# A planner that knows the SBUF port shared by VectorE and GpSimd, and three gate blocks early, two held back

## The chip, the cores and the metric

The kernel runs on one core of a Trainium2 chip. The metric is the device time of one execution, in microseconds. Names used below: TensorE (PE in the profile) multiplies matrices and transposes, VectorE (DVE) and ScalarE (ACT) do elementwise work, GpSimd (POOL) does elementwise work too, and SyncE (SP) issues nearly all DMA transfers.

## The reference

One encoder block over a sequence of 1024 positions and 1024 channels, in float32.

```python
h = rmsnorm(x, norm_w) * (1 + scale) + shift          # scale, shift, gate from silu(c) @ w_ada
proj = h @ w_in                                       # split into the parts below
ya = (a_cg * dwconv3(a_bg * a_x) * silu(a_z)) @ w_pa
q, k, v = split(silu(dwconv5(concat(q, k, v))))       # 8 heads of 128 channels
q, k = l2norm(q), l2norm(k)
o = gated_delta(q, k, v, g, beta) + flip(gated_delta(flip(q), flip(k), flip(v), ...))
yb = (headnorm(o) * gdn_norm_w * silu(z_b)) @ w_pb
merged = sigmoid(gate_a_raw) * ya + sigmoid(gate_b_raw) * yb
y = rmsnorm(x + gate * (merged @ w_o), final_norm_w)
```

The gated delta rule updates a 128x128 state per head and direction, chunk by chunk. In a chunk it needs the inverse of a lower triangular matrix that is built from the products of the keys.

## The kernel before

Every large product is made from a high and a low part of both factors: three matmuls (high by high, high by low, low by high) for each of eight 128-row slices, on halves of 512 positions. A *block* is the product of 128 output channels for all 1024 positions, 48 matmuls. Its weights arrive by DMA in two pieces; ScalarE rounds each to the high part (`wh_...`) and GpSimd subtracts to get the low part (`wl_...`).

The kernel has three stages.

1. The start: x is loaded, normalised, transposed and modulated; the first blocks k0, q0, v0 are made. In the profile this is about the first 99 us.
2. The heads, to about 821 us. For each head h: blocks q, k, v and z of the input projection; a five-tap convolution of q, k and v on VectorE (`conv5`, 1024 columns per instruction) and a Silu on ScalarE; `prep_k` (transposes `ktp`, decay matrices `D`, products `gram`, the matrices `N`); the inversion of the 32x32 diagonal blocks on GpSimd, 60 short instructions on tiles `E` and `et` with data brought in and out by DMA (`N<-s`, `Vb<-s`); `merge` (transposes of `N` and `Vb` into `T`, `y`, products `psy`, `psu`, `psz`, `psv`), which joins the blocks to 128x128 inverses; `prep_q` (`qk`, `qtp`, `vtp`); `chain`, eight steps in two directions at once, each step running cb, r (VectorE), cb, vw (ScalarE), cb, S (VectorE); the normalisation of the output (`oss`, `vp`) and `head_out` (`otp`, and a store).
3. The rest, written in program order: four blocks of gate b, the gated convolution mixer, the output products, the last norm.

In the first two stages the order of instructions is planned when the program is built. Generators (`chain`, `merge`, `head_out`, `prep_k`, `prep_q`, and `fill` for the blocks) yield their TensorE instructions; every VectorE, ScalarE, GpSimd and DMA instruction is recorded as an `Op` with an estimated cost (`Engine.cost`) and its dependences. `Scheduler.run` keeps an estimated clock for TensorE (`t`) and a time at which each other engine is free (`free`), and always issues what can start first; among instructions that are ready on an engine, the one with the smaller priority number and older number goes first. The resulting order on every engine is fixed. On the chip each engine runs its queue in that order and waits where an operand is late. TensorE takes the streams in the order in which they are listed, chains first and blocks last.

`fill` decides which block comes next, one block ahead of the one in work:

```python
share = (total - START - RESERVE) * (mains - len(jobs)) / mains + START
if gates and jobs and total - len(gates) < int(share):
    return gates.pop(0)
if jobs and (len(gates) <= RESERVE or all(n in sched.done for n in jobs[0][3])):
    return jobs.pop(0)
return gates.pop(0) if gates else None
```

`gates` are eight blocks of gate a, ga0 to ga7 (a Sigmoid on ScalarE and a store follow each). `jobs` are 27 blocks of the heads, in the order k2, v1, z0, then q, k, v, z for the heads that follow (q2, k3, v2, z1, and so on), and at the end q7, v7, z6, z7. Each has conditions: q and k wait for a chain two heads back, v for the queries of the head before, z for a head's output. With START = 4 and RESERVE = 4 the order is q1, ga0 to ga3, all 27 jobs, ga4 to ga7.

The functions that the change touches, with what calls them:

Of the kernel before, what the change touches and what calls it, by code (L numbers as in the profile page):

```python
# [21 lines left out]
NEG = -1.0e30  # L22

A_BG, A_CG, A_X, A_Z, Q0, K0, V0, Z0, G_A, G_B = (8 * i for i in range(10))
START = 4
RESERVE = 4
PLAIN = (0, 4)
LAST = 6
AHEAD = 5
# [9 lines left out]


class Op:
    def __init__(self, engine, issue, cost, extra, table, prio, seq):
        self.engine, self.issue, self.cost, self.extra, self.table = engine, issue, cost, extra, table
        self.key, self.ready, self.left, self.after = (prio, seq), 0.0, 0, []


# [8 lines left out]
class Scheduler:  # L55
# [9 lines left out]
    def __init__(self, pe):  # L65
        self.pe, self.t, self.prio, self.seq = pe, 0.0, 2, 0
        self.where, self.count, self.slots = {}, {}, {}
        self.free, self.queue, self.table, self.waiting = {}, {}, None, 0
        self.done, self.held, self.busy = set(), set(), {}

    @contextmanager
# [36 lines left out]
        parts = [self.slots[slot, i] for i in range(4) if (slot, i) in self.slots]  # L108
        return not any(s.reads or s.writes or s.fills for s in parts)

    def record(self, engine, issue, outs, ins, cost, extra, table, fill):
        op = Op(engine, issue, cost, extra, table, self.prio, self.seq)
        self.seq += 1
        op.reads = [s for ap in ins for s in self.parts(ap)]
        op.writes = [s for ap in outs for s in self.parts(ap)]
        op.fill = fill
        deps = set()
        for s in op.reads:
            op.ready = max(op.ready, self.after(engine, s.write, s.fill))
            deps.update(s.writes, s.fills)  # L120
        for s in op.writes:
            op.ready = max(op.ready, self.after(engine, s.read, s.fill))
            deps.update(s.reads, s.fills)
            if fill:
                op.ready = max(op.ready, self.after(engine, s.write))
                deps.update(s.writes)
        op.left = len(deps)
        for d in deps:
            d.after.append(op)
        for s in op.reads:  # L130
            s.reads.append(op)
        for s in op.writes:
            (s.fills if fill else s.writes).append(op)
        self.waiting += 1
        if not op.left:
            self.queue.setdefault(engine, []).append(op)

    def issue(self, op, at):
        load = 1.28 if op.table and op.table != self.table else 0.0
        self.table = op.table or self.table  # L140
        op.issue()
        self.free[op.engine] = at + op.cost + load
        end = at + op.cost + load + op.extra
        for s in op.reads:
            s.reads.remove(op)
            s.read[op.engine] = max(s.read.get(op.engine, 0.0), end)
        for s in op.writes:
            if op.fill:
                s.fills.remove(op)
                s.fill[op.engine] = max(s.fill.get(op.engine, 0.0), end)  # L150
            else:
                s.writes.remove(op)
                s.write[op.engine] = max(s.write.get(op.engine, 0.0), end)
        for d in op.after:
            d.left -= 1
            d.ready = max(d.ready, end + self.hop(op.engine, d.engine))
            if not d.left:
                self.queue.setdefault(d.engine, []).append(d)
        self.waiting -= 1
# [102 lines left out]
class Engine:  # L262
# [4 lines left out]

    def cost(self, op, outs, ins, kw):

        n = outs[0].free_size() / 1000.0  # L270
        if self._name == "dma":
            size = min(outs[0].nbytes(), ins[0].nbytes())
            return max(0.4, size / 360e3), 2.4 + size / 500e3
        if self._name == "act":
            pointers = sum(isinstance(kw.get(k), bass.AP) for k in ("bias", "scale"))
            return 0.1 + 0.83 * n + 0.07 * pointers + 0.12 * (len(outs) > 1), 0.08
        if self._name == "pool":
            if ALU.pow in kw.values():
                return 1.7, 0.1
            return (0.31 + 1.95 * n if "tensor" in op else 0.06 + 0.7 * n), 0.05  # L280
        if op == "transpose":
            return 0.16 + 1.1 * n, 0.03
        both = sum(i.space != PSUM and i.free_size() == outs[0].free_size() for i in ins) > 1
        fast = op in ("tensor_copy", "tensor_scalar", "memset") and ins and ins[0].space != PSUM
        return 0.07 + 0.06 * (op == "scalar_tensor_tensor") + (0.66 if fast else 1.16 if both else 1.04) * n, 0.07

    def __getattr__(self, op):
        real = getattr(self._engine, op)

        def call(*args, **kw):  # L290
            aps = [x for x in args if isinstance(x, bass.AP)]
            outs = aps[:1] + [kw[k] for k in ("out", "accum_out") if k in kw]
            ins = aps[1:] + [v for k, v in kw.items() if k not in ("out", "accum_out") and isinstance(v, bass.AP)]
            outs = [o for o in outs if o is not None]
            table = next((x for x in args if x in (AF.Silu, AF.Exp, AF.Sigmoid)), None) if self._name == "act" else None
            cost, extra = self.cost(op, outs, ins, dict(enumerate(args), **kw))
            self._sched.record(self._name, lambda: real(*args, **kw), outs, ins, cost, extra, table, op == "memset")  # L297

        return call

# [2 lines left out]
def block(ctx: ExitStack, tc: tile.TileContext, x, cT, wada, wadag, badaT, nwT, win, wab, cva, cvq,  # L303
# [773 lines left out]
    def fill():  # L1077
# [14 lines left out]
        def choose():  # L1092
# [6 lines that stand above are left out]
# [501 lines left out]
```

## Time and profile before

| | us |
|---|---|
| median of 3 runs | 1506.59 |
| lowest and highest of them | 1505.53, 1507.33 |
| the profiled execution, its own time | 1503.92 |
| its span, first to last instruction | 1502.1 |
| busy in the span: TensorE | 1409.6 |
| VectorE | 856.0 |
| ScalarE | 612.3 |
| GpSimd | 678.8 |

The busy time of an engine is the time in which at least one of its instructions runs. "PEclk", and the column after the engines in a table by stage, is the clock that TensorE was granted, as a part of full speed. In rows of groups, "x8 | 17.2, 2150 | 35.9" means eight instructions, 17.2 us of busy time together, 2150 ns each in the mean, and 35.9 us in which the engine stood idle just before them. In rows of waits, the numbers are the total in us, the count and the longest. In rows of the timeline, the first number is the start in us, the second the duration, and a bracket gives the idle time before it and what ended it; "x2" is two instructions merged into one row.

### The profile page before, as it was taken

To read this page: it belongs to the slowest core of one execution; us is meant where nothing else is said; L and a number is where in the kernel's file an instruction comes from. 1 tells how busy PE (TensorE), PEld (TensorE's weight loads), DVE (VectorE), ACT (ScalarE), POOL (GpSimd) and SP (SyncE) were. 2 spreads that over 40 slices of the span, in tenths; PEclk is the share of its full clock that TensorE was granted. 3 is DMA by queue.
4 is the path that set the end of the run, shared out by engine and by line. 5 is a ranking of instruction groups with operands and counts; after the bars stand their busy time and mean duration, and the time that the engine had idled before them with its cause. 6 is when DMAs were issued, how large, how long until landed. Compare 5 with 4: busy or idle time off the path is not lost.

```text
span 1502.1 us, 22636 instructions
## 1 busy us (share of the span) xinstructions
PE 1409.6 (94%) x8526; PEld 1164.2 (78%) x8526; DVE 856.0 (57%) x1467; ACT 612.3 (41%) x1493; POOL 678.8 (45%) x864
## 2 busy tenths in 40 slices
PE   4899898999899898989999999999999999999998
PEld 3777677878678786868787878787877787788886
DVE  6969075575656757476424636575667455623335
ACT  5229636456554646365433332222222341222211
POOL 5213756635637273643713554455555412255301
PEclk9999899999999999999999999999999999999999
DMA  8323241224122232323212220303031276655502
GB/s 300 99 88 105 74 131 32 82 72 127 43 72 80 51 108 49 95 71 99 56 44 85 98 99 29 112 28 113 29 106 35 93 258 229 225 191 168 197 14 99
DMA packets 123581, 153.37 MB, mean 102 GB/s; under 512 B 74704, under 2 KB 75088, under 8 KB 123472
## 3 DMA queue, kind: packets, MB, share of 16 engines
q1 hardware_dynamic: 123184, 151.14, 31.6%
q8 instruction: 67, 1.10, 0.3%
q10 hardware_dynamic: 288, 0.79, 0.1%
q14 instruction: 42, 0.34, 0.1%
HBM read 122.40 MB, written 29.49 MB: 101 GB/s over the span
## 4 chain that ended last, share of the span: by engine, by line
PE 44%; DVE 7%; POOL 2%; ACT 2%; issue 1%; POOLq 0%; ACTq 0%
PE ps_ax_S L1233 3%; PE ps_cg_S L1233 3%; PE pp_ga L206 3%; PE ps_bg_S L1233 3%; PE ps_az_S L1233 2%; PE pp_pb L1137 2%; PE pp_pb L1138 2%; PE pp_pb L1139 2%; PE fo L1506 2%; PE fo L1504 2%; PE fo L1505 2%; DVE ga L1438 2%; PE pp_gb L1137 1%; PE pp_gb L1138 1%; PE pp_gb L1139 1%; PE ps_ax_A L1233 1%
## 5 line engine op out<-in xcount | busy, mean ns | idle before, releaser
L297 POOL TENSOR_TENSOR et<-E 128x30 f32<-128x30 f32 (+7 forms) x240 | 111.3, 464 | 26.7 <-DMA E<-s 9.4
L297 POOL TENSOR_TENSOR E<-E,et 128x30 f32<-128x30 f32 (+7 forms) x240 | 109.6, 457 | 17.8
L297 ACT ACTIVATE vw<-cb,cols 128x128 f32<-128x128 f32 x112 | 35.7, 365 | 114.7 <-PE cb L206 114.6
L297 DVE SCALAR_TENSOR_TENSOR S<-S,exps,cb 128x128 f32<-128x128 f32 x96 | 29.3, 342 | 80.8 <-PE cb L206 80.2
L297 DVE SCALAR_TENSOR_TENSOR N<-gram,cols,D 128x128 f32<-128x128 f32 x128 | 34.6, 342 | 48.1 <-PE gram L206 48.1
L297 POOL TENSOR_TENSOR wl_q<-wr_q,wh_q 128x512 fp32r<-128x512 f32 x16 | 24.0, 1504 | 77.9 <-ACT wh_q L297 71.6
L206 PE MATMUL pp_ga<-hhi,wh_ga 128*128 128x512 f32 x128 | 53.2, 415 | 5.0 <-ACT wh_ga L297 5.0
L1129 POOL TENSOR_TENSOR wl_pa<-wr_pa,wh_pa 128x512 fp32r<-128x512 f32 x16 | 20.7, 1310 | 80.7 <-ACT wh_pa L1128 80.7
L206 PE MATMUL pp_z<-hhi,wh_z 128*128 128x512 f32 x128 | 55.0, 430 | 0.0
L206 PE MATMUL pp_z<-hlo,wh_z 128*128 128x512 f32 x128 | 54.4, 425 | 0.0
L206 PE MATMUL pp_z<-hhi,wl_z 128*128 128x512 f32 x128 | 54.0, 422 | 0.0
L206 PE MATMUL pp_ga<-hhi,wl_ga 128*128 128x512 f32 x128 | 53.0, 414 | 1.0 <-POOL wl_ga L297 0.8
L297 POOL TENSOR_TENSOR wl_ga<-wr_ga,wh_ga 128x512 fp32r<-128x512 f32 x16 | 22.9, 1441 | 68.4 <-PE pp_ga L206 33.2
L206 PE MATMUL pp_ga<-hlo,wh_ga 128*128 128x512 f32 x128 | 52.7, 412 | 0.0
L297 ACT ACT_TABLE_LOAD x40 | 51.3, 1283 | 1.4 <-PEq L1595 0.8
L1137 PE MATMUL pp_pb<-bhi,wh_pb 128*128 128x512 f32 x128 | 50.6, 396 | 0.0
L1139 PE MATMUL pp_pb<-bhi,wl_pb 128*128 128x512 f32 x128 | 50.6, 395 | 0.0
L1138 PE MATMUL pp_pb<-blo,wh_pb 128*128 128x512 f32 x128 | 50.6, 395 | 0.0
L1137 PE MATMUL pp_pa<-yhi,wh_pa 128*128 128x512 f32 x128 | 50.5, 394 | 0.0
L1138 PE MATMUL pp_pa<-ylo,wh_pa 128*128 128x512 f32 x128 | 49.9, 389 | 0.0
L1139 PE MATMUL pp_pa<-yhi,wl_pa 128*128 128x512 f32 x128 | 49.8, 389 | 0.0
L297 DVE SCALAR_TENSOR_TENSOR r<-cb,negeg,vp 128x128 f32<-128x128 f32 x112 | 34.4, 345 | 25.9 <-PE cb L206 25.0
(807 smaller groups left out, 4695.7 us busy)
## 6 DMA issues: line engine op xcount, KB each, us to landing
wada<-in_wada SPq DMA_DIRECT2D x16, 512.0 KB, 6.9
D<-gr_d SPq DMA_DIRECT2D x16, 512.0 KB, 5.9
xt<-in_x SPq DMA_DIRECT2D x8, 512.0 KB, 8.3
wr_k<-in_win SPq DMA_DIRECT2D x16, 256.0 KB, 3.3
wr_q<-in_win SPq DMA_DIRECT2D x16, 256.0 KB, 3.7
wr_v<-in_win SPq DMA_DIRECT2D x16, 256.0 KB, 4.3
wr_ga<-in_win SPq DMA_DIRECT2D x16, 256.0 KB, 3.0
qg<-er_d SPq DMA_DIRECT2D x8, 512.0 KB, 5.5
```

The lines of the kernel that those rows point to most:

```text
L206: getattr(self.pe, what)(out, *ins, **kw)
L297: self._sched.record(self._name, lambda: real(*args, **kw), outs, ins, cost, extra, table, op == "memset")
L1129: G.tensor_tensor(lo[:, ch(q, 512)], raw, hi[:, ch(q, 512)].bitcast(F32), ALU.subtract)
L1137: PE.matmul(ps, wh, mhi[k][:, sl], start=i == 0, stop=False)
L1138: PE.matmul(ps, wh, mlo[k][:, sl], start=False, stop=False)
L1139: PE.matmul(ps, wl, mhi[k][:, sl], start=False, stop=i == KT - 1)
L1233: PE.matmul(ps, w[:, ch(m)], r, start=first and m == i == 0, stop=m == 3 and i == 2, skip_group_check=True)
L1438: V.scalar_tensor_tensor(ga, wt[:, d, :], sc_t[:, d : d + 1], ga, ALU.mult, ALU.add)
L1504: PE.matmul(ps, mhi[k][:, ch(t)], wh, start=k == 0, stop=False)
L1505: PE.matmul(ps, mlo[k][:, ch(t)], wh, start=False, stop=False)
L1506: PE.matmul(ps, mhi[k][:, ch(t)], wl, start=False, stop=k == KT - 1)
```

## The change

The planner gets one time for the shared port, `Scheduler.port`. An instruction that uses the port starts no earlier than that time and moves it to its own end. On GpSimd every instruction of more than 30 columns uses it, but memsets and powers do not. On VectorE an instruction of more than 30 columns uses it if it has two full-size SBUF inputs, or if it is a copy or an operation with scalars on one SBUF input. The cost constants of GpSimd and of VectorE's two-input instructions are set anew. START goes from 4 to 3 and RESERVE from 4 to 2. What the kernel computes, its instructions and their sizes stay as they are; only their order can differ.

```diff
-START = 4
-RESERVE = 4
+START = 3
+RESERVE = 2
...
 class Op:
-    def __init__(self, engine, issue, cost, extra, table, prio, seq):
-        self.engine, self.issue, self.cost, self.extra, self.table = engine, issue, cost, extra, table
+    def __init__(self, engine, issue, cost, extra, table, port, prio, seq):
+        self.engine, self.issue, self.cost, self.extra, self.table, self.port = engine, issue, cost, extra, table, port
...
-        self.free, self.queue, self.table, self.waiting = {}, {}, None, 0
+        self.free, self.queue, self.table, self.waiting, self.port = {}, {}, None, 0, 0.0
...
         op.issue()
+        if op.port:
+            at = max(at, self.port)
+            self.port = at + op.cost
         self.free[op.engine] = at + op.cost + load
         end = at + op.cost + load + op.extra
...
         if self._name == "dma":
             size = min(outs[0].nbytes(), ins[0].nbytes())
-            return max(0.4, size / 360e3), 2.4 + size / 500e3
+            return max(0.4, size / 360e3), 2.4 + size / 500e3, False
         if self._name == "act":
             pointers = sum(isinstance(kw.get(k), bass.AP) for k in ("bias", "scale"))
-            return 0.1 + 0.83 * n + 0.07 * pointers + 0.12 * (len(outs) > 1), 0.08
+            return 0.1 + 0.83 * n + 0.07 * pointers + 0.12 * (len(outs) > 1), 0.08, False
         if self._name == "pool":
             if ALU.pow in kw.values():
-                return 1.7, 0.1
-            return (0.31 + 1.95 * n if "tensor" in op else 0.06 + 0.7 * n), 0.05
+                return 1.62, 0.1, False
+            return (0.28 + 1.93 * n if "tensor" in op else 0.06 + 0.7 * n), 0.05, op != "memset" and n > 0.03
         if op == "transpose":
-            return 0.16 + 1.1 * n, 0.03
+            return 0.16 + 1.1 * n, 0.03, False
         both = sum(i.space != PSUM and i.free_size() == outs[0].free_size() for i in ins) > 1
         fast = op in ("tensor_copy", "tensor_scalar", "memset") and ins and ins[0].space != PSUM
-        return 0.07 + 0.06 * (op == "scalar_tensor_tensor") + (0.66 if fast else 1.16 if both else 1.04) * n, 0.07
+        return (0.07 + 0.06 * (op == "scalar_tensor_tensor") + (0.66 if fast else 1.08 if both else 1.04) * n, 0.07,
+                bool(both or fast) and n > 0.03)
```

`record` and `__getattr__` hand the new value `port` from `cost` to `Op`. `n` is the number of columns in thousands.

More of the change, by code (lines that the diff above doesn't have):

```diff
@@ L109, in clear, with record @@
         return not any(s.reads or s.writes or s.fills for s in parts)
-    def record(self, engine, issue, outs, ins, cost, extra, table, fill):
-        op = Op(engine, issue, cost, extra, table, self.prio, self.seq)
+    def record(self, engine, issue, outs, ins, cost, extra, table, fill, port):
+        op = Op(engine, issue, cost, extra, table, port, self.prio, self.seq)
         self.seq += 1
@@ L295, in call @@
             table = next((x for x in args if x in (AF.Silu, AF.Exp, AF.Sigmoid)), None) if self._name == "act" else None
-            cost, extra = self.cost(op, outs, ins, dict(enumerate(args), **kw))
-            self._sched.record(self._name, lambda: real(*args, **kw), outs, ins, cost, extra, table, op == "memset")
+            cost, extra, port = self.cost(op, outs, ins, dict(enumerate(args), **kw))
+            self._sched.record(self._name, lambda: real(*args, **kw), outs, ins, cost, extra, table, op == "memset", port)
         return call
```

## The prediction

> **What bounds the kernel now.** I read the page first, then busy time by stage, then what TensorE waited for, then the timeline of the engines around each long wait.
>
> ```profile
> span 1502.1 us, 22636 instructions
> PE 1409.6 (94%) x8526; PEld 1164.2 (78%) x8526; DVE 856.0 (57%) x1467; ACT 612.3 (41%) x1493; POOL 678.8 (45%) x864
> ...
> 0.00:99.00 99.00, 73.48 (x338) 59.62 (x338) 71.74 (x156) 34.92 (x55) 30.22 (x43) 0.97 0.43 151
> 99.00:821.00 722.00, 667.53 (x5268) 562.62 (x5267) 424.77 (x860) 391.01 (x1117) 366.29 (x611) 0.96 0.29 81
> 821.00:1502.00 681.00, 668.59 (x2925) 541.93 (x2923) 359.49 (x452) 186.36 (x321) 282.30 (x210) 1.00 0.34 118
> ```
>
> TensorE is the bound. The amount of its work is fixed, so the time can only change by what it loses. The change reorders the first two stages (0 to 99, and the heads, 99 to 821); the third is written in program order and stays. In the heads TensorE is idle for 722 - 667.5 = 54.5 us and its granted clock is 0.96. What it waited for, over the span:
>
> ```profile
> PE ktp L206 <- ACT kT L297: 8.3, 2, 5.1
> ...
> PE cb L206 <- DVE S L297: 7.5, 3, 6.6
> PE psy L206 <- ACT sqj L297: 7.3, 1, 7.3
> PE otp L206 <- DVE vp L297: 5.6, 3, 2.7
> PE pp_ga L206 <- ACT wh_ga L297: 5.0, 1, 5.0
> ...
> PE psm L206 <- DVE acc L297: 4.1, 3, 2.4
> ```
>
> Every engine runs a fixed order worked out from estimated durations. A TensorE instruction that has to wait holds up everything behind it, even where product matmuls were ready. So the long waits mark places where the estimate was too early. Four of them carry 8.3 + 6.6 + 7.3 = 22.2 us (ktp has two).
>
> Why was the estimate early? The same four GpSimd forms, first beside an idle VectorE, then beside VectorE's convolution, and what followed:
>
> ```profile
> 243.14 0.28 POOL L297 TENSOR_TENSOR et<-E 128x56 f32<-128x56 f32 x1
> 243.50 0.31 POOL L297 TENSOR_TENSOR E<-E,et 128x56 f32<-128x56 f32 x1
> 243.88 0.26 POOL L297 TENSOR_TENSOR et<-E 128x42 f32<-128x42 f32 x1
> 244.22 0.27 POOL L297 TENSOR_TENSOR E<-E,et 128x42 f32<-128x42 f32 x1
> ...
> 393.29 1.20 POOL L297 TENSOR_TENSOR et<-E 128x56 f32<-128x56 f32 x1
> 394.57 1.27 POOL L297 TENSOR_TENSOR E<-E,et 128x56 f32<-128x56 f32 x1
> 395.91 1.26 POOL L297 TENSOR_TENSOR et<-E 128x42 f32<-128x42 f32 x1
> 397.25 1.27 POOL L297 TENSOR_TENSOR E<-E,et 128x42 f32<-128x42 f32 x1
> ...
> 393.06 2.60 DVE L297 SCALAR_TENSOR_TENSOR kT<-xpad,cvq_t,kT 128x1024 f32<-128x1024 f32 x2
> ...
> 404.97 0.43 DVE L297 STREAM_TRANSPOSE T<-N 32x256 f32<-32x256 f32 x1 [6.59 <-DMA N<-s]
> ...
> 407.99 0.84 ACT L297 ACTIVATE T<-Vb 32x256 f32<-32x256 f32 x2 [8.51 <-DMA Vb<-s]
> ```
>
> Four instructions took 5.0 us in place of 1.12, 3.9 us late. E's result comes back by DMA to VectorE's transposes and ScalarE's copies, which stood too early in their queues and sat 6.59 and 8.51 us with ready work behind them. ScalarE's squares of ktp were among it, and psy waited 7.3 us for them. The other three places:
>
> ```profile
> 252.11 0.88 DVE L297 STREAM_TRANSPOSE T<-N 32x256 f32<-32x256 f32 x2 [7.26 <-DMA N<-s]
> ...
> 256.76 0.60 DVE L297 SCALAR_TENSOR_TENSOR S<-S,exps,cb 128x128 f32<-128x128 f32 x2
> ...
> 481.75 1.87 DVE L297 TENSOR_SCALAR kT<-xpad,cvq_t 128x1024 f32<-128x1024 f32 x1
> ...
> 565.16 0.31 DVE L297 TENSOR_SCALAR vp<-vp,oss 128x128 f32<-128x128 f32 x1 [4.51 <-POOL oss L297]
> ...
> 567.79 2.30 DVE L297 SCALAR_TENSOR_TENSOR kT<-xpad,cvq_t,kT 128x1024 f32<-128x1024 f32 x1
> ```
>
> At 252 the chain's state update S stands behind transposes that wait for a late E. At 482 and 568 kT's own steps are stretched (2.30 against 1.30 each at 393), and at 565 the queue stood 4.51 us for a GpSimd power behind a late E. All four places are the shared port.
>
> **The change, part by part.** *Port in the estimate, and refitted costs.* No instruction is added or removed. The bound above is all four waits, 22.2 us, plus the clock they cost afterwards:
>
> ```profile
> 250.00:300.00 50.00, 41.73 (x446) 35.83 (x445) 30.88 (x78) 18.84 (x58) 27.14 (x52) 0.93 0.30 80
> 400.00:450.00 50.00, 40.45 (x426) 33.62 (x425) 27.72 (x73) 26.40 (x76) 17.63 (x26) 0.90 0.32 75
> 450.00:500.00 50.00, 46.33 (x366) 38.60 (x366) 35.89 (x61) 26.09 (x87) 31.32 (x55) 0.97 0.26 75
> 550.00:600.00 50.00, 44.07 (x428) 36.06 (x427) 36.66 (x76) 32.62 (x102) 23.91 (x39) 0.93 0.33 88
> ```
>
> Against full clock these stretches miss (0.07 + 0.10 + 0.03 + 0.07) x 50 = 13.5 us. Part of that falls on time in which TensorE stood anyway, so I take half, 7. Upper bound 22.2 + 7 = 29 us. Below nothing too: a new order of 860 + 1117 + 611 instructions of VectorE, ScalarE and GpSimd makes new misses, and I bound that by the worst single miss of now with its clock, 7.3 + 5 = 12 us lost. I take half of the upper end, 14.5 us gained. The value lies nearer the upper end because each of the four traces back to one cause that the new estimate carries. It is not the whole, since what is late next stays: ScalarE's weight casts (5.0 us before pp_ga) and VectorE's vp before otp (5.6 us).
>
> *The first stage.* The same estimate orders it, and VectorE's sums and GpSimd's scalings share the port there. The nearest row is psm waiting 4.1 us for acc: between 4 gained and 4 lost, and I take 0.
>
> *Three gate blocks early.* One block of 48 matmuls leaves the place before k2. What TensorE ran into there, the 5.0 us wait for weights that ScalarE casts late, now stands before k2's weights: 0. No cover goes missing, because k2, v1 and z0 need nothing late and move up.
>
> *Three blocks in the middle.* The rule takes a gate when the next job's condition is not met at the moment of choosing and more than two gates are left; choosing happens one job ahead. The places in time:
>
> ```profile
> 229.92 0.40 PE L206 MATMUL pp_z<-hhi,wh_z 128*128 128x512 f32 x1
> ...
> 262.04 0.49 PE L206 MATMUL o<-vn,D 128*128 128x128 f32 x2
> ...
> 636.09 0.39 PE L206 MATMUL pp_v<-hhi,wh_v 128*128 128x512 f32 x1
> ...
> 811.19 0.63 PE L206 MATMUL otp<-ident,vp 128*128 128x128 f32 x3 [2.06 <-DVE vp L297]
> ...
> 820.91 0.39 PE L1137 MATMUL pp_gb<-hhi,wh_gb 128*128 128x512 f32 x1
> ...
> 832.07 0.39 PE L1137 MATMUL pp_gb<-hhi,wh_gb 128*128 128x512 f32 x1
> ```
>
> A block costs 832.07 - 820.91 = 11.2 us. z0 begins at 229.9 while chain 0 runs until 262. q2 needs chain 0, so at that choice a gate is taken, and at the next choice, z0's end, another. By a third choice, some 20 us later with a chain step between, chain 0 should be over; the third gate waits for a later unmet condition (z7 needs head 6's output). So five gates stand ahead of q2 in place of four: everything from q2 to k7 comes 11.2 us later, less what the first term saves. The gate's own extras, a Sigmoid table load on ScalarE and a store on SP's queue, happen wherever it stands: 0.
>
> *Two blocks held back.* From the end of k7's product (636.09) to head 7's last transposes (811.19, done at 812.0) take 176 us. TensorE has that time covered now by v6, z5, q7, v7, z6, z7 and 3.2 of the four gates; 820.9 - 812.0 = 8.9 us of gates follow. Head 7's way through E, merge, chain and output is not made of product matmuls, so I keep its 176 us. Then the tail ends at 812.0 + 11.2 = 823.2 with nothing behind it, against 820.9: 2.3 us lost, and TensorE idles where the gates were. A shorter way, with fewer weight casts in GpSimd's and ScalarE's queues, would gain; I take 0.
>
> **Sum:** -14.5 + 2.3 = -12.2 us. The profiled execution took 1503.9 us around a span of 1502.1, so it would become 1491.7. The median of the runs shown is 1506.6, 2.7 higher; from there the forecast is **1494.4 us**.
>
> **A rule beside a row.** Short instructions are left out of the new port: 0.03 thousand columns is the limit, and powers have none. The powers in the heads:
>
> ```profile
> L297 POOL TENSOR_TENSOR kss<-kss,pos_half 128x8 f32<-128x8 f32 x8 | 17.2, 2150 | 35.9 <-DVE kss L297 35.5 <-DVE qss L297 0.3
> ...
> L297 POOL TENSOR_TENSOR oss<-oss,pos_half 128x8 f32<-128x8 f32 x8 | 14.1, 1759 | 27.5 <-DVE oss L297 27.5
> ```
>
> They average 2.15 and 1.76 us for the same 8 columns, against the 1.62 that the estimate now holds: 8 x 0.53 + 8 x 0.14 = 5.4 us unplanned. If such powers keep the place at 565 as it is (5.1 us, and with half of its 3.5 us of clock 6.9), the upper bound falls to 22, its half to 11, and the time is 1498. The Trainium skill, "SBUF — State Buffer", section "SBUF: two separate sides", says that the shared pair of ports is an exclusive lock for a whole instruction, between a GpSimd instruction and any VectorE one in a two-port mode or with two SBUF inputs, and gives no size below which it is free. By that rule the 1498 holds, and the trace's 2.15 us agrees.
>
> **The rivals.**
> *All of it comes back.* The four waits go, with their clock, and so do smaller ones: -29 + 2.3 gives about 1480. For it: one cause in all four. Against it: ScalarE, whose waits the change leaves. Chance 0.17.
> *The change doesn't do what it says.* The new order misses as much elsewhere, since queues still run in order: 0 + 2.3, 1509; with a few us saved, 1504 to 1509. For it: in a chain of eight heads one late result moves all that follow. Chance 0.15.
> *Slower: the tail loses its cover.* If chain 0 is still open at the third choice, six gates stand ahead of q2, k7 is 22.4 us later and two blocks less lie after it: the tail ends at 812.0 + 22.4 = 834.4, 13.5 us lost. That decides as soon as the ports bring back less than 13.5 us; at a half of my 14.5, 7, it gives 1513. For it: chain 0 closed 32 us after z0 began, and an estimate with the port makes it longer still. Against it: 6.6 us of those were the wait for S. Chance 0.2.
> *The likeliest:* 1485 to 1503.5. Chance 0.48, of which 0.15 is for the short instructions' 1498.
>
> **How the numbers follow.** About 0.2%, 3 us, can be told from no change here. Faster: 0.48 + 0.17 and a little of the mixed case, 0.67; within 0.2%: 0.13; slower: 0.20. The range goes to 1479 and to 1513, which leaves out about 0.1 on each side; the likeliest one's own range is 1485 to 1503.5.
>
> **What would show it.** Right: between 99 and 800 TensorE's waits for kT, S and sqj fall below half of 22 us, the transposes T<-N stand behind VectorE work that was ready, and the granted clock of the heads rises above 0.96. GpSimd's E instructions keep their 1.2 us beside convolutions, because the port is only foreseen, not freed. Three gates stand before k2, two between z0 and q2, two after z7; the last stage keeps its 681 us; TensorE shows idle time in the last 60 us of the heads. Wrong: waits of the same total at other tiles (ports not the cause, or not foreseen well), or more than 14 us of idle time after the last gate (the tail).

## The result, and the profile after

The changed kernel takes 1463.3 us (median; 1459.5 to 1468.9) against 1506.1 for the kernel before (1504.1 to 1507.3): a ratio of 0.972, 95% interval 0.9687 to 0.9754. It is 43 us faster, where I had forecast 12 and allowed up to 28.

Both profiled executions, cut at the same places: the first product of k1, the last of k7, the first of gate b. The columns are the stretch, its length, the busy time of PE, PEld, DVE, ACT and POOL, PE's granted clock, the DMA share and GB/s. Before:

```profile
0.00:99.30 99.30, 73.78 (x338) 59.89 (x339) 72.04 (x156) 34.94 (x56) 30.22 (x43) 0.97 0.43 151
99.30:635.80 536.50, 493.25 (x3920) 415.76 (x3919) 329.46 (x663) 298.96 (x857) 292.36 (x503) 0.96 0.30 85
635.80:820.90 185.10, 173.88 (x1346) 146.51 (x1346) 95.02 (x197) 92.02 (x262) 73.93 (x109) 0.97 0.24 69
820.90:1502.00 681.10, 668.69 (x2925) 542.01 (x2923) 359.49 (x452) 186.36 (x321) 282.30 (x210) 1.00 0.34 118
```

After:

```profile
0.00:94.20 94.20, 72.21 (x320) 58.49 (x321) 67.19 (x141) 33.91 (x53) 29.45 (x43) 0.82 0.46 165
94.20:610.40 516.20, 494.42 (x3963) 419.40 (x3962) 339.55 (x667) 301.06 (x861) 294.15 (x491) 0.99 0.33 93
610.40:777.20 166.80, 157.55 (x1322) 135.87 (x1321) 90.50 (x201) 81.53 (x253) 78.93 (x121) 0.96 0.20 55
777.20:1457.80 680.60, 668.36 (x2925) 542.20 (x2924) 364.44 (x459) 187.09 (x322) 285.56 (x210) 1.00 0.34 119
```

The first stage is 5.1 us shorter, the stretch to k7 20.3, the tail 18.3, the rest 0.5: 44.2 of span. The lengths alone mislead, because work has moved across the second cut. Six gates stand ahead of k7 instead of four, which is 22.4 us more at 11.2 us a block. Other products went the other way: two blocks are 96 matmuls, and the count to k7 rises by 43 only (3920 to 3963). So I compare what TensorE lost. Its idle time, length less busy time, fell from 43.2 to 21.8 us in the stretch to k7, from 11.2 to 9.3 in the tail, and from 92.4 to 65.3 in all. The other 17.1 us are busy time of the same matmuls (1409.6 to 1392.5), which goes with the granted clock: to k7 it rose from 0.96 to 0.99. Most of the gain lies between k1 and k7.

Cut once more at the first product of q2, the part from q2 to k7, before and then after:

```profile
262.80:636.00 373.20, 347.09 (x2929) 295.11 (x2917) 228.97 (x481) 197.26 (x601) 202.08 (x352) 0.96 0.29 78
```

```profile
266.60:610.80 344.20, 331.28 (x2910) 282.94 (x2909) 234.27 (x472) 198.28 (x593) 202.35 (x337) 1.00 0.32 90
```

This part is 29 us shorter, though no gate stands in it in either run. Some of that is work that moved: 104 short products of the chains (`cb`, `o`) now stand behind k7. But TensorE's idle time in the part falls from 26.1 to 12.9 us and its clock rises from 0.96 to 1.00; from k1 to q2 the idle time falls from 17.1 to 8.9. The change put gates ahead of q2, and the larger part of the gain arises behind it.

TensorE's waits in that stretch after (total, times, longest):

```profile
PE pp_ga L209 <- ACT xpad L302: 4.5, 1, 4.5
PE psz L209 <- ACT T L302: 4.1, 3, 1.7
PE cb L209 <- ACT N L302: 2.8, 1, 2.8
...
PE ktp L209 <- ACT kT L302: 1.1, 1, 1.1
```

Of the four places, ktp's waits went from 8.3 to 1.1 us; S and the squares of ktp are gone from the list. The prediction traced them to VectorE's transposes (`T<-N`) and ScalarE's copies (`T<-Vb`), which stand in their queues and wait for E's result by DMA. These waits over the whole span, before and then after:

```profile
ACT T L297 <- DMA Vb<-s: 29.1, 5, 8.5
DVE T L297 <- DMA N<-s: 25.1, 8, 7.3
```

```profile
DVE T L302 <- DMA N<-s: 7.3, 6, 2.2
ACT T L302 <- DMA Vb<-s: 1.2, 2, 1.1
```

The lock itself is still there: an instruction of the one engine takes longer beside one of the other. GpSimd and VectorE in the timeline after:

```profile
413.78 0.25 POOL L302 TENSOR_TENSOR E<-E,et 128x30 f32<-128x30 f32 x1
414.11 1.28 POOL L302 TENSOR_TENSOR et<-E 128x15 f32<-128x15 f32 x1
415.47 1.32 POOL L302 TENSOR_TENSOR E<-E,et 128x15 f32<-128x15 f32 x1
...
414.04 1.27 DVE L302 SCALAR_TENSOR_TENSOR vT<-xpad,cvq_t,vT 128x1024 f32<-128x1024 f32 x1
```

Beside a convolution, 15 columns take 1.3 us; 30 columns just ahead of it took 0.25. The planner does not hold these, as both have 30 columns or fewer. What is new is where the gates stand:

```profile
189.75 0.40 PE L209 MATMUL pp_z<-hhi,wh_z 128*128 128x512 f32 x1
...
201.79 0.40 PE L209 MATMUL pp_ga<-hhi,wh_ga 128*128 128x512 f32 x1
...
262.62 0.38 PE L209 MATMUL o<-vn,D 128*128 128x128 f32 x2
...
266.57 0.40 PE L209 MATMUL pp_q<-hhi,wh_q 128*128 128x512 f32 x1
```

z0 begins at 189.8 (229.9 before) and is done at 201.8, chain 0 ends at 262.6 as before, and q2 follows at 266.6. Between z0's end and q2's condition lie 61 us. Three gates stand there beside the chain's products, and TensorE is busy for 58.0 of them.

### The profile page after: what moved, and what is told of

Same layout as the page of the kernel before. It is cut to its first block, busy times and chain, and to the rows that moved or that the text cites. A ratio compares the mean times of both kernels' runs of the same rounds, so it can differ in the third digit from the quotient of the medians.

```text
span 1457.8 us, 22609 instructions
## 1 busy us (share of the span) xinstructions
PE 1392.5 (96%) x8526; PEld 1156.0 (79%) x8526; DVE 861.7 (59%) x1467; ACT 603.6 (41%) x1488; POOL 688.1 (47%) x864
## 4 chain that ended last, share of the span: by engine, by line
PE 70%; DVE 12%; ACT 7%; DMA 4%; POOL 4%; issue 3%; SPq 2%; POOLq 0%; ACTq 0%
PE pp_ga L209 4%; PE pp_k L209 4%; PE cb L209 4%; PE pp_v L209 4%; PE ps_ax_S L1238 3%; PE ps_cg_S L1238 3%; PE o L209 3%; PE ps_bg_S L1238 3%; PE pp_q L209 3%; PE ps_az_S L1238 2%; PE pp_pb L1142 2%; PE pp_pb L1144 2%; PE pp_pb L1143 2%; PE fo L1509 2%; PE fo L1511 2%
## 5 line engine op out<-in xcount | busy, mean ns | idle before, releaser
L302 POOL TENSOR_TENSOR E<-E,et 128x30 f32<-128x30 f32 (+7 forms) x240 | 119.6, 498 | 17.6
L1143 PE MATMUL pp_pa<-ylo,wh_pa 128*128 128x512 f32 x128 | 49.8, 389 | 0.0
L302 DVE SCALAR_TENSOR_TENSOR kT<-xpad,cvq_t,kT 128x1024 f32<-128x1024 f32 x32 | 46.5, 1455 | 0.4
L209 PE MATMUL pp_q<-hhi,wl_q 128*128 128x512 f32 x112 | 46.4, 414 | 0.0
```

Of the source, the lines that this page charges most:

```text
L209: getattr(self.pe, what)(out, *ins, **kw)
L1143: PE.matmul(ps, wh, mlo[k][:, sl], start=False, stop=False)
```

## The experiments

Three things were changed at once: the port's rule, the refitted constants, and the places of the gates. START and RESERVE only bound those places; the planner picks the moment, so runs with the same two numbers can differ in "gates ahead of q2". Theory A: the port in the estimate carries the gain. Rival B: the places of the gates do. Rival C: any new order scatters, and this one was lucky. After the first runs A became A': the port and the gates pay only together. Rival D came up beside it: any estimate that is long enough does. "Idle to k7" is, for each run, the length of the stretch from the first product of k1 to the last of k7 less TensorE's busy time in it, from one row by stage as above. The ratio is to the kernel before on the same chip, whose median was 1503.2 to 1506.1.

| | port | constants | gates ahead of q2 | us | ratio to before, 95% | idle to k7, us | clock there |
|---|---|---|---|---|---|---|---|
| before | no | old | 4 | 1506.1 | 1 | 43.2 | 0.96 |
| after | yes | new | 6 | 1463.3 | 0.969 to 0.975 | 21.8 | 0.99 |
| port_gates44 | yes | new | 4 | 1498.2 | 0.994 to 0.997 | 42.9 | 0.97 |
| gates_alone | no | old | 5 | 1496.8 | 0.993 to 0.996 | 44.9 | 0.96 |
| costs_alone | no | new | 4 | 1518.7 | 1.008 to 1.011 | 49.3 | 0.95 |
| after_noport | no | new | 5 | 1524.1 | 1.011 to 1.015 | 52.6 | 0.96 |
| after_noport_nudge | no | new | 5 | 1523.9 | 1.012 to 1.018 | 54.6 | 0.96 |
| before_s6r2 | no | old | 6 | 1512.8 | 1.003 to 1.008 | 46.7 | 0.95 |
| before_nudge | no | old | 4 | 1514.1 | 1.004 to 1.010 | 46.4 | 0.95 |
| after_mean_wait | its mean | new | 6 | 1492.7 | 0.990 to 0.996 | 31.5 | 0.96 |
| after_nudge | yes | new | 6 | 1482.0 | 0.983 to 0.989 | 24.7 | 0.98 |
| after_nudge2 | yes | new | 6 | 1462.0 | 0.969 to 0.974 | 20.7 | 0.99 |
| after_s6r2 | yes | new | 6 | 1475.8 | 0.978 to 0.982 | 29.6 | 0.98 |
| after_s4r2 | yes | new | 6 | 1478.7 | 0.982 to 0.987 | 25.9 | 0.99 |
| after_s3r5 | yes | new | 3 | 1521.9 | 1.007 to 1.018 | 53.9 | 0.94 |
| after_s3r1 | yes | new | 7 | 1506.3 | 1.000 to 1.002 | 36.5 | 0.97 |
| after_oldcosts | yes | old | 6 | 1504.1 | 0.998 to 1.001 | 33.2 | 0.97 |
| after_short_ops | yes, all sizes | new | 6 | 1493.6 | 0.991 to 0.994 | 34.5 | 0.97 |
| gate_before_z7 | yes | new | 6 | 1463.0 | 0.971 to 0.975 | 20.8 | 0.98 |

**The parts one by one.** The changed planner with the gates as before:

```diff
 # the changed kernel
-START = 3
-RESERVE = 2
+START = 4
+RESERVE = 4
```

> The changed planner (port and refitted costs) with the gate blocks where they were before (START 4, RESERVE 4). Theory A, the port in the estimate carries the gain: about 30 of the 43 us come, 1470 to 1480, and TensorE's waits for kT, S and the squares of ktp are mostly gone. Rival B, the places of the gates carry it: 1495 to 1507. Rival C, any new order scatters by luck: anywhere from 1460 to 1510, with waits of the old size at other tiles.

Measured: 1498.2, a gain of 6 us (against 1504.2 beside it). That is 18 us above A's range, and in B's. The waits for kT, S and the squares of ktp are gone from the long ones, as A said (23.1 us in all before, 3.8 here), but TensorE stands as much as before, elsewhere. One such place:

```profile
232.47 0.75 PE L209 MATMUL cb<-vw,ktok 128*128 128x128 f32 x4 [1.01 <-ACT vn L302]
236.35 0.88 PE L209 MATMUL cb<-r,N 128*128 128x128 f32 x4 [1.46 <-DVE r L302]
238.97 1.30 PE L209 MATMUL cb<-vw,ktok 128*128 128x128 f32 x4 [1.73 <-ACT vn L302]
...
255.61 0.48 PE L209 MATMUL pp_q<-hhi,wh_q 128*128 128x512 f32 x1
```

These are rows of TensorE's timeline in this run. z0 is done, q2 may not start before chain 0 ends, and the chain's steps run bare: a wait in several steps, then q2 at 255.6. The four gates that are left are held back, so the plan has no block to put in. But this gap is not the main loss: TensorE idles for 6.1 of the 40 us between z0's end and q2. The same run from k1 to q2, and from q2 to k7:

```profile
96.00:255.60 159.60, 146.01 (x959) 121.58 (x958) 98.00 (x176) 93.32 (x251) 85.97 (x153) 0.97 0.33 96
255.60:626.30 370.70, 341.40 (x2920) 289.12 (x2918) 237.71 (x495) 203.01 (x605) 196.65 (x333) 0.97 0.30 83
```

TensorE idles 13.6 us in the first part and 29.3 in the second; in the changed kernel it is 8.9 and 12.9. The second part takes 344 us there in place of 371, and its work is the same but for eight short products of the chain. So with the port planned for, two gates more ahead of q2 are worth most behind q2, where neither run has a gate. What carries that over is not shown. Later blocks come some 11 us later against the work of the other engines (q2 at 266.6 for 255.6), which may give that work a lead, but no run tests it.

The gates with the old planner:

```diff
 # the kernel before
-START = 4
-RESERVE = 4
+START = 3
+RESERVE = 2
```

> The old planner with START 3 and RESERVE 2. Theory A: the gates alone bring at most 13 us, 1493 to 1510, and the four long waits stay in another shape. Rival B: 1463 to 1480. Rival C: anywhere from 1460 to 1510.

Measured: 1496.8, a gain of 7. In A's range; B, which needs 1463 to 1480 here, is out as well. The waits keep their size: psy still waits for the squares of ktp, 10.5 us in one piece.

The constants alone, and the changed kernel without the port:

```diff
 # the changed kernel; for costs_alone also START = 4, RESERVE = 4
-        if op.port:
+        if False:
             at = max(at, self.port)
```

> The refitted costs without the port, gates as before (4 and 4). The two-input costs of VectorE fall by 0.08 per thousand columns, so the estimate of a convolution step falls from 1.32 to 1.24 us while the chip takes 1.28 alone: theory A expects 1500 to 1515, no better than before, since the lock's waits are planned even less. Rival C: anywhere from 1460 to 1510.

> The changed kernel without the port's rule in the issue step; refitted costs, START 3 and RESERVE 2 stay. Theory A: the gain is lost for the most part, 1490 to 1510. Rival B: 1463 to 1475, as the changed kernel. Rival C: anywhere from 1460 to 1510.

Measured: 1518.7 and 1524.1. Both are slower than before. As I read it, with smaller constants and no port the estimate of a held instruction is shorter still; the waits of VectorE's and ScalarE's T for E's result are 63.3 and 53.9 us, against 54.2 before. A's expectation of the second, up to 1510, was too good. In this pair the gates bring nothing (5 us lost) and the port's rule is worth 61 us (1524.1 to 1463.3); with four gates it is worth 20 (1518.7 to 1498.2). Both figures are for the new constants, and the 61 includes one gate more ahead of q2. With the old constants and the new gates the rule brought nothing in the one order that was run: 1496.8 without it, 1504.1 with it (after_oldcosts, below).

**Is it luck?** Edits without meaning, which only draw another order:

```diff
 # after_nudge: the changed kernel; before_nudge: the kernel before, 1.95 to 1.94
-            return (0.28 + 1.93 * n if "tensor" in op ...
+            return (0.28 + 1.94 * n if "tensor" in op ...
 # after_nudge2: the changed kernel; after_noport_nudge: the kernel without the port
-HOPS = {'same': -0.05, 'other': 0.2, 'from pe': 0.4, 'to pe': 0.35}
+HOPS = {'same': -0.05, 'other': 0.2, 'from pe': 0.41, 'to pe': 0.35}
```

> The changed kernel with one cost constant of GpSimd moved by half a per cent (1.93 to 1.94 per thousand columns): an edit without meaning that gives another order. Theory A (the planner foresees the port, and the free gates fill what it foresees): 1458 to 1475. Rival C (the order that won is one lucky draw): 1475 to 1510.

> The kernel before with the same kind of nudge (1.95 to 1.94): another order of the old planner. Theory A: 1495 to 1520, on the old level. Rival C: anywhere from 1460 to 1520.

> The changed kernel with a hop of TensorE's results estimated 0.41 us in place of 0.40: a second edit without meaning. Theory A': up to k7's end the loss stays near 30 to 35 us as in the changed kernel and its first nudge (67 before), and the tail scatters: 1460 to 1485. Rival C: above 1490.

> The changed kernel without the port's rule, with the same edit without meaning as the second nudge (0.40 to 0.41). Theory A': again on the level without the port, 1495 to 1530, long waits and half clock of 60 or more up to k7. Rival C: anywhere from 1460 to 1530.

Measured: 1482.0, 1514.1, 1462.0 and 1523.9. An order's draw is worth up to 19 us, more than my whole forecast. The first lies outside A's range (1482 for 1458 to 1475). So part of the 43 us is luck: the refitted port planner with six gates ahead of q2 and two behind gained 21 to 44 us in five orders (1462 to 1482: after, two nudges, two other splits of the gates). Luck alone is out, since the plans without any port came to 1497 to 1524 in seven orders. That group of five is a narrow one: with old constants, or with short instructions in the port, the same gates gave 1504.1 and 1493.6 (below). To k7, where the gain lies, the two nudges agree with the changed kernel in TensorE's idle time (24.7, 20.7 and 21.8):

```profile
95.20:607.80 512.60, 487.86 (x3831) 413.10 (x3830) 325.59 (x645) 304.97 (x840) 282.61 (x460) 0.98 0.31 87
607.80:798.60 190.80, 171.91 (x1455) 147.59 (x1454) 99.71 (x224) 89.43 (x281) 84.78 (x151) 0.96 0.24 66
```

These are the first nudge's rows by stage, to k7 and the tail. Its tail holds 133 matmuls more than that of the changed kernel (1455 for 1322), so the lengths do not compare; the idle times do. To k7 it is 24.7 us for 21.8, in the tail 18.9 for 9.3: most of what it lost is lost in the tail.

**The gates' number and place, with the port.**

```diff
 # the changed kernel, START and RESERVE of 3 and 2 become
+# after_s3r5: 3, 5     after_s6r2: 6, 2     after_s4r2: 4, 2     after_s3r1: 3, 1
```

> The changed kernel with three gates early, none in the middle and five held back. If the three middle gates are what makes the port's knowledge pay (rival B in part), this is close to the port with 4 and 4: 1490 to 1505. If fewer early gates are enough: 1458 to 1475.

> The changed kernel with all six free gates early (START 6, RESERVE 2), none while chain 0 runs. Theory A' (the plan with the port foresees TensorE's waits during chain 0, and gates are what can stand there): k2, v1 and z0 come 33 us later instead and stand there themselves, so the loss up to k7 stays near that of the changed kernel, 1458 to 1490. If the middle place as such counts: 1490 to 1520.

> The changed kernel with four gates early, two in the middle, two held back: six ahead of q2 as in the changed kernel. Theory A': a loss of 25 to 50 up to k7's end and 1458 to 1485. Rival C (1463 is one lucky draw among even odds): above 1490.

> The changed kernel with one gate held back instead of two. In the changed kernel TensorE loses about 10 us (long waits and half clock) between the end of z6 and z7, which waits for head 6's output; a fourth free gate should go there, and the tail then has one gate less behind z7. If cover at that place is what lacks: 1452 to 1460. If the tail needs both gates at its end: 1464 to 1472. A new order alone moves it by up to 20 either way (the nudged kernel came to 1482).

Measured: 1521.9, 1475.8, 1478.7 and 1506.3. With three gates ahead of q2 and none behind z0 the port planner is slower than the kernel before, beyond what I had expected. There the gap costs its full price: in the 66.8 us from z0's end to q2 TensorE idles for 25.0, at a granted clock of 0.80. The waits of T for E's result are back as well, 49.8 us in all, though the port is planned for. With six ahead of q2 the place hardly counts: six early or four and two come to 1476 and 1479, inside the nudges' scatter. The seventh did harm in the one order that was run. TensorE's waits in that run:

```profile
PE vtp L209 <- ACT vT L302: 30.3, 5, 8.3
PE otp L209 <- DVE vp L302: 12.0, 4, 9.4
```

and a stretch around one of them:

```profile
510.00:525.00 15.00, 6.65 (x37) 5.68 (x36) 5.58 (x14) 14.84 (x25) 8.67 (x16) 0.83 0.26 74
```

In each of four heads TensorE waits 6.5 to 8.3 us for vT, which stands in ScalarE's queue, and in the stretch shown ScalarE is busy for 14.84 of 15 us. I had expected the place ahead of z7 to be filled; the rule took the fourth free gate at q2 instead.

The same six early gates with the old planner:

```diff
 # the kernel before
-START = 4
-RESERVE = 4
+START = 6
+RESERVE = 2
```

> The old planner with all six free gates early and two held back, the same order of blocks as the run of the changed planner that came to 1476. Theory A' (gates pay because the port is planned for): no gain from them without the port, 1498 to 1525. Rival B (the order of blocks alone does it): 1470 to 1485.

Measured: 1512.8, as A' expected. The two kernels make their blocks in the same order, and the planner alone, port and constants, makes 37 us between them (1512.8 to 1475.8). This is the cleanest pair for the planner: the gates' places are the same. Old planner, then changed planner, to k7:

```profile
98.50:656.80 558.30, 511.64 (x3989) 430.00 (x3988) 329.75 (x659) 309.85 (x861) 280.51 (x490) 0.95 0.30 85
```

```profile
94.20:624.50 530.30, 500.69 (x3961) 424.31 (x3961) 334.06 (x668) 306.55 (x864) 289.40 (x487) 0.98 0.32 91
```

The stretch is 28 us shorter, TensorE's idle time in it 46.7 and 29.6 us.

**What of the port counts.** Its mean in place of its rule, the old constants with it, and short instructions in it:

```diff
 # the changed kernel; after_mean_wait, with `if op.port` off
+                0.28 + 1.93 * n + 0.13 * (n > 0.03)                                     # GpSimd
+                ... * n + 0.07 * (bool(both or fast) and n > 0.03)                      # VectorE
 # after_oldcosts: 1.62, 0.28 + 1.93 n, 1.08 become
+                1.7, 0.31 + 1.95 n, 1.16
 # after_short_ops
-                return 1.62, 0.1, False      op != "memset" and n > 0.03      bool(both or fast) and n > 0.03
+                return 1.62, 0.1, True       op != "memset"                   bool(both or fast)
```

> The changed kernel with the port's rule replaced by its mean: each GpSimd instruction of over 30 columns is estimated 0.13 us longer and each port instruction of VectorE 0.07 us longer, no port time. Theory A (what counts is which instruction is held, and when): 1485 to 1515. Rival D (any estimate that is long enough does): 1460 to 1475.

> The changed kernel with the old cost constants: port and gates without the refit. Theory A': the old constants hold 0.08 per thousand columns too much for two-input instructions, so the port is planned a little too long, 1460 to 1485. If the refit is a needed third part: 1490 to 1510.

> The changed kernel in which short instructions and powers use the port as well. Theory A with the short instructions worth what I put on them (up to 7 us): 1455 to 1463. If they do not matter, only the order's scatter: 1463 to 1485.

Measured: 1492.7, 1504.1 and 1493.6. D's range (1460 to 1475) is missed, but the mean alone brings 31 us against the kernel without port and mean (1524.1), where the rule brings 61. Each is one order, and the kernel without has five gates ahead of q2 in place of six. The old constants lose the whole gain. Where:

```profile
95.20:620.30 525.10, 491.90 (x3831) 414.35 (x3830) 323.55 (x650) 293.03 (x833) 277.77 (x460) 0.97 0.30 85
620.30:821.20 200.90, 175.36 (x1455) 150.78 (x1453) 96.85 (x222) 90.62 (x282) 84.42 (x151) 0.94 0.24 65
```

This order has the same number of matmuls on either side of k7 as the first nudge (3831 and 1455), so I compare it with that run. It takes 12.5 us longer to k7 (525.1 for 512.6) and 10.1 longer in the tail (200.9 for 190.8). To k7 TensorE idles for 33.2 us, more than in any refitted order with six gates ahead of q2 (20.7 to 29.6). That speaks for the constants, but one order does not tell them from the draw, so whether the refit is a needed third part stays open. The short instructions' version is 30 us slower than the changed kernel, 11 more than the nudge lost; 10.4 of them lie ahead of k1, which starts at 104.6 us in place of 94.2. With the port over the powers too, the estimate may be too long, but that was not tried apart.

**What sets the tail.**

```diff
 # the changed kernel, in choose()
+            if len(jobs) == 1 and len(gates) == RESERVE:
+                return gates.pop(0)
             share = ...
```

> The changed kernel with the seventh gate ahead of z7 instead of behind it; the plan up to z6 is the same. In the changed kernel TensorE loses about 10 us between z6 and z7, and has both gates behind z7. If head 7's own way (E, merge, chain, output) sets the end of the heads, as I assumed with my 176 us: 1459 to 1467, no gain, the lost time only moves. If TensorE's work sets it: 1450 to 1457.

Measured: 1463.0, no gain. The changed kernel's rows, then this run's:

```profile
714.72 0.26 PE L209 MATMUL psy<-T,N 32*32 32x32 f32 x1 [4.12 <-ACT vp L302]
...
774.88 1.61 PE L209 MATMUL otp<-ident,vp 128*128 128x128 f32 x8 [0.68 <-DVE vp L302]
```

```profile
777.19 1.94 PE L209 MATMUL otp<-ident,vp 128*128 128x128 f32 x8 [5.54 <-DVE vp L302]
```

The gate went into the gap ahead of z7, and the lost time came back at the end: head 7's last transposes now wait 5.54 us for vp with nothing else to do, and start 2.3 us later than they did (1.8 of it because k7 ends that much later in this run). From k7's end on, both runs take the same time, 167 us: here head 7's own way sets the tail, not the place of TensorE's work.

## Why the prediction was wrong

**The direction was right, and so was the place of the misses.** In the eleven runs that plan with the port, TensorE's waits for kT, S and the squares of ktp sum to 3.8 us at most; in the seven plans without any port they come to 4.2 to 23.1 (the mean wait alone brings them to 1.7). E's instructions kept their 1.2 to 1.3 us. The last stage kept its 681 us, and the clock to k7 rose from 0.96 to 0.99.

**The step that failed is the sum of two separate terms,** "-14.5 + 2.3 = -12.2 us". It took the port's gain and the gates' price to be independent, and each term fails when it is measured alone. With the gates as they were, port and refit gained 6 us, not 14.5. With the old planner the gates gained 7 us, where I had put a loss of 2.3. Together they gained 43. The runs with six gates ahead of q2 show the same with less luck in it: 21 to 44 us gained with the port and the refit, 9 lost without (before_s6r2, 1512.8 for 1504.0).

**In the port's term the bound was the wrong quantity.** I built its upper end from four waits, 22.2 us and 7 of clock. With the port and the old gates these waits went, and TensorE idled for 42.9 us to k7 in place of 43.2: a wait that is removed is not time gained, as long as TensorE next stands elsewhere. In after_noport_nudge they are down to 4.2 us, and it is among the slowest runs, at 1523.9. As an upper end for the whole change 29 us was too low, too. The row of the heads showed 54.5 us idle and a clock of 0.96 over 722 us (another 29 at most), and that loss is the most that a new order could reach.

**In the gates' term I looked at cover to be paid for.** My sentence "No cover goes missing" looked at the gates that leave one place and not at what work ahead of q2 does for the rest. The gap that the plan now shows behind z0 is one part (25.0 us idle where nothing stands in it); the larger part lies behind q2, and its mechanism stays open.

**The third choice came out the other way:** chain 0 was still open, so six gates stand ahead of q2, which was my rival on the slower side (-7 + 13.5, 1513). Its premise held and its price did not. From k7's end to head 7's last transposes it took 166 us, not 176 (610.6 to 776.5), and k7 came 25 us earlier instead of later. "The tail loses its cover" did not cost 13.5 us: TensorE idles for 9.3 us there, 11.2 before. That the tail's end is set by head 7's own way agrees with gate_before_z7; that its length is fixed does not hold: the stretch from k7's end to gate b took 163 to 201 us in these runs, with somewhat different work in it.

**The size of the 43 us is partly luck.** In the order of the first nudge the same edit takes 1482.0 us, inside my range. Another constant without meaning would have hidden the error in the sum.

**The first stage** came out 5.1 us shorter where I took 0 and bounded it at 4, with 18 matmuls fewer ahead of the cut; TensorE's idle time in it fell from 25.5 to 22.0 us.

**The short instructions:** nothing in the runs shows that leaving them out of the port costs anything here. The row of 2.15 us for a power stands, but the planner that holds all sizes and powers came to 1493.6.

## What to carry to other kernels

Where a fixed order is planned from estimated durations, a resource that two engines share belongs into the estimate as a resource, with a time at which it is free; a mean added to every instruction brought half as much here, in one order each. Do not book a wait that goes as time gained: look at where the engine stands next. Here the port's knowledge paid only together with independent work placed ahead (6 us alone, 43 with it), so look for such work in the same edit, and judge the two together. And before one order is called better, nudge a constant that means nothing: here that alone moved the time by up to 19 us, almost half of what the edit had gained.

## What the runs showed of the hardware

The two sides of the lock are unequal. While VectorE runs convolution steps back to back, GpSimd gets about one instruction in for each of them, 1.2 to 1.3 us for 15 to 56 columns, while the steps beside it hardly stretch: 1.27 us each after, 2.60 for two before. The weight casts are the other way round: behind one of GpSimd's, VectorE's instruction took 2.30 us. In the whole trace before, a convolution step (`scalar_tensor_tensor`, 1024 columns) that overlaps only E's instructions takes 1.46 us at most, one that overlaps a cast up to 2.38; alone it takes 1.27 to 1.29.

TensorE's clock can be low without the stage getting longer. The first stage after has a granted clock of 0.82, against 0.97 before, and is still 5.1 us shorter. From 20 to 40 us it has half the clock throughout:

```profile
20.00:40.00 20.00, 13.88 (x55) 11.02 (x56) 17.69 (x32) 8.33 (x16) 12.21 (x11) 0.50 0.68 261
```

TensorE is still idle for 6.1 of these 20 us, waiting for VectorE and ScalarE, so it does not set the pace there.
